# The opening of a decoder layer: identity transposes while x loads, a shorter bias table with its block part copied on VectorE, earlier row factors, and a DRAM spread cut in 16 pieces

## Chip, cores and metric

The kernel runs on one core of one Trainium2 chip. The metric is device time in microseconds (us) of one execution; lower is better. Runs of one kernel differ a little, so times are compared as medians of several.

## The reference

One layer of a decoder with S = 512 tokens and D = 2048 columns, batch 1, all in float32. A normalized input goes through an attention mixer with 16 heads in 4 groups, is added back, and a SwiGLU block (2048 to 2 x 5632 and back) follows, with a last norm:

```python
hn = rmsnorm(h, mix_norm_g[i])
h = h + nsa_mixer(hn, rel_bias, nsa_w_in[li], nsa_w_out[li], ...)
h = h + swiglu(rmsnorm(h, ffn_norm_g[i]), ffn_w_in[i], ffn_w_out[i])
return rmsnorm(h, final_norm_g)
```

The mixer projects hn to queries, to keys and values of three branches (compressed blocks, selected blocks, window) and to gates. Keys and values of the compressed branch go through a small MLP over blocks of 32 tokens with stride 16. Each score gets a bias that depends on the head and on a bucket of the distance between query and key: `rel_bias[rel_bucket(dist)]`, with 32 buckets. With 512 tokens every block is selected and the window covers all, so selected and window branches both see all keys up to the query.

## The kernel before, in words

All matrix products are split in two parts each: a value x becomes a high part (a rounded copy, ACT) and a low part (x minus the high part, VectorE, called DVE in the profile), and `three` (L264) issues three matmuls for a product: high x high, low x high, high x low (L265 to L267).

**Weights.** The class `Weights` (L63) holds a list of weight pieces, most of 512 KB, in the order of use. `load` (L72) issues a DMA on SP into one of three `raw` buffers; `split` (L82) makes `whi` on ACT (L95) and `wlo` on VectorE (L96) in one of four buffers; `take` gives out the next piece and `ahead(n)` splits until n pieces are ready, then issues loads until three more are on their way. A load can go out only when the split of the piece three places before has freed its `raw` buffer. Every engine works through its own instructions in the order in which the program lists them.

**Opening (L360 to L480).** The input x is loaded as four tiles of 128 tokens, in four column quarters, on SP and ACT's queue. PE transposes x into chunks of 128 columns (16 chunks in all). Each chunk is scaled by the norm's gain: ACT makes `hn_h` (L400), VectorE `hn_l` (L401). The row factor of the norm (one over the root mean square of a token) isn't applied here; it is multiplied into the outputs of the projections. The first four chunks are made before the first projection (L439, then `scaled_in`). The first projection (`ws`, 24 matmuls for a weight piece) then runs in four quarters `q`; in quarters 0 to 2 the next four chunks are made between its matmuls (`chunk`, L392), so each chunk is used one quarter later. The table `side` names further work of a quarter:

- `square(i)` (L406): ACT squares half a token tile and sums it, for the row factors; eight of them.
- `pos_turn`: two small transposes.
- `table(c0, c1)` (L414): the bias table `tab`, made by a matmul of the 33 x 16 biases with a one-hot matrix `oh` and copied by VectorE. Columns 0 to 639 hold the bias for the distances 511 down to -128; 16 x 62 further columns hold, for each of 16 offsets b, the distances 465 + b - 16 n. They are made in four parts of 512, 128, 496 and 496 columns.
- `factors` (L419): a chain of small VectorE instructions with one Sqrt on ACT; it ends with `diag` (L429), a diagonal matrix of the row factors.

After quarter 3, PE multiplies ones by `diag` (L468), and ACT copies the result to `ybc` (L469), the row factors of all tokens in every partition. Then POOL writes `tab` to DRAM (`d_t`, L472, and `d_c`, L473), reads the compressed branch's bias back in eight DMAs (L475), and issues the spread: `d_u` (L479) gets 128 copies of the 10240 values of `d_t`, in four DMAs of 2560 columns. Much later each head's bias tile `tb` is read from `d_u` by one DMA on SP (L726).

**Then** (L533 to L550): the second and third projection of 256 columns each (4 weight pieces each), and a loop of four turns, each with one projection piece (`ws`) and two pieces of the first MLP (`mlp1`), all of which pass through `Weights`. The text calls this loop the first MLP stretch. Behind it come the other projections, the attention, the output product and the SwiGLU block, which the change doesn't touch.

PSUM tiles of the opening come from `bank`, which takes turns between the names "tr" and "mlp", two buffers each.

Of the kernel before, what the change touches and what calls it, by code (L numbers as in the profile page):

```python
# [10 lines left out]
F32 = mybir.dt.float32  # L11
F32R = mybir.dt.float32r
I32 = mybir.dt.int32
AF = mybir.ActivationFunctionType
# [24 lines left out]
TP_GAP, HN_GAP = 40, 48  # L39
RESYNC = 14  # L40
SPREAD = 2560


def _bucket_onehot():
# [127 lines left out]
def nsa_block(ctx: ExitStack, tc: tile.TileContext, x, rel_bias, mix_g, ffn_g, fin_g, w_in, w_out,  # L172
# [111 lines left out]
    def run(gen):  # L284
        for _ in gen:
            pass
# [61 lines left out]
    with ExitStack() as st1:  # L348
# [4 lines left out]
        def proj_tiles(n=2):  # L353
            return [(ps1 if next(turns) % 4 > 1 else psx).tile([128, 512], F32, name="proj") for _ in range(n)]
# [5 lines left out]
        with ExitStack() as st0:  # L360
# [3 lines left out]
            g16 = xp.tile([KC, 128], F32, name="g16")  # L364
            gcol = xp.tile([128, KC], F32, name="gcol")
            relt = xp.tile([NB + 1, H], F32, name="relt")
            oh = xp.tile([NB + 1, UL + 16 * CL], F32, name="oh")
            ones = xp.tile([128, 128], F32, name="ones")
            diag = xp.tile([128, NT, 128], F32, name="diag")
            nc.scalar.dma_start(g16, mix_g.rearrange("o (k p) -> (o k) p", p=128))  # L370
            for q in range(4):
                if q < RAW:
                    W.load()
                for t in range(NT):
                    eng = nc.scalar if q < 2 and t % 2 else nc.sync
                    eng.dma_start(xt[t][:, 512 * q:512 * (q + 1)], x[tok(t), 512 * q:512 * (q + 1)])
                if q == 0:
                    act(warm, epsc, AF.Sqrt)
                if q == 1:
                    nc.sync.dma_start(oh, onehot)  # L380
            pool.dma_start(pos[:, 0], pos_k)
            pool.dma_start(pos[:, 1], pos_v)
            pool.dma_start(relt[:NB, :], rel_bias)
# [5 lines left out]
            def bank(shape):  # L389
                return ps1.tile(shape, F32, name=next(names))  # L390
# [13 lines left out]
            def square(i):  # L404
                t, c = i % NT, i // NT
                act(junk, xt[t][:, 1024 * c:1024 * (c + 1)], AF.Square, accum_out=ssq[:, t, c:c + 1])  # L406
# [7 lines left out]
            def table(c0, c1):  # L414
                p = bank([H, 512])
                mm(p[:, :c1 - c0], relt, oh[:, c0:c1], start=True, stop=True)
                dve.tensor_copy(tab[:, c0:c1], p[:, :c1 - c0])

            def factors():  # L419
# [9 lines left out]
                dve.tensor_tensor(diag, ident.unsqueeze(1).to_broadcast([128, NT, 128]),  # L429
                                  ymul.unsqueeze(2).to_broadcast([128, NT, 128]), op=OP.mult)  # L430

            p = bank([128, KC])
            nc.tensor.transpose(p, g16, ident[:KC, :KC])
            dve.tensor_copy(gcol, p)
# [5 lines left out]
            for k in range(4):  # L440
                scaled_in(k, ps[k])
            ps = proj_tiles()
            cuts = ((0, 512), (512, UL), (UL, UL + 496), (UL + 496, UL + 992))
            side = [[lambda: square(0)], [pos_turn, lambda: square(1), lambda: square(2), lambda: table(*cuts[0])],
                    [lambda: square(3), lambda: square(4), lambda: table(*cuts[1]), lambda: square(5),
                     lambda: table(*cuts[2]), lambda: table(*cuts[3])],
                    [lambda: square(6), lambda: square(7), factors]]
            for q in range(4):
                it = ws(ps, q, W.take(0))
                next(it)  # L450
                if q < 3:
                    W.split()
                else:
                    W.ahead(1)
                for f in side[q]:
                    f()
                for _ in range(4):
                    next(it)
                if q == 3:
                    W.ahead(2)  # L460
                for k in range(4 * q + 4, 4 * q + 8):
                    if q < 3:
                        chunk(k)
                    if k % 4 < 3:
                        next(it)
                run(it)
            p = bank([128, S])
            mm(p, ones, diag.rearrange("p t c -> p (t c)"), start=True, stop=True)  # L468
            act(ybc, p, AF.Copy)  # L469
            ps_kc0 = ps  # L470
            W.ahead(3)
            pool.dma_start(d_t, tab[:, :UL])  # L472
# [1 line left out]
            for a in range(8):  # L474
                pool.dma_start(biasc[16 * a:16 * a + 16],  # L475
                               bass.AP(tensor=d_c.tensor, offset=d_c.offset + 7 - a,
                                       ap=[[CL, 16], [16 * CL, H], [1, 55]]))
            for c0 in range(0, H * UL, SPREAD):
                pool.dma_start(d_u[:, c0:c0 + SPREAD], bass.AP(tensor=d_t.tensor, offset=d_t.offset + c0,  # L479
                                                               ap=[[0, 128], [1, SPREAD]]))  # L480

        cp = st1.enter_context(tc.tile_pool(name="cp", bufs=1))
        blk_h = cp.tile([128, 32, G, 32], F32R, name="blk_h")
# [10 lines left out]
        def kv_out(ps, g0):  # L494
            return lambda u: dve.tensor_tensor(kvT[:, g0 + u], ps[u], ybc, op=OP.mult)
# [11 lines left out]
        def mlp1(ps, gi, g):  # L507
            for k in range(4):
                i = 4 * gi + k
                three(ps, blk_h[:, i].rearrange("p g c -> p (g c)"), blk_l[:, i].rearrange("p g c -> p (g c)"),  # L510
                      g[0][:, k], g[1][:, k], i == 0, i == 31)
# [21 lines left out]
        ps = proj_tiles()  # L533
        for i in range(4):
            run(ws(ps, i, W.take(), end=kv_out(ps, 2)))
        ps = proj_tiles()
        for i in range(4):
            run(ws(ps, i, W.take()))
            build_blk(0, i)
        W.ahead(3)  # L540
        for u in range(2):
            kv_out(ps, 0)(u)
        ps, hk = proj_tiles(), ps1.tile([128, 256], F32, name="mlp")
        for i in range(4):
            run(ws(ps, i, W.take(), end=kv_out(ps, 2)))
            mlp1(hk, 2 * i, W.take())
            mlp1(hk, 2 * i + 1, W.take())
        W.ahead(3)
        hid = gelu(hk)
        ps = proj_tiles()  # L550
# [883 lines left out]
```

## Time and profile before

| what | value |
|---|---|
| time, median of 3 runs | 2171.51 us (2167.26 to 2173.09) |
| profiled execution, its own time | 2174.41 us |
| its span | 2172.7 us |
| granted TensorE clock, mean | 0.996 |
| busy: PE, weight loads, VectorE, ACT, POOL | 2141.7, 1984.1, 1580.9, 928.3, 54.5 us |
| DMA traffic | 344.14 MB, mean 158 GB/s |

The profile is of one execution. A row of the timeline gives start and duration in us, engine, line, instruction, what it writes and reads, how many were merged, and in square brackets how long the engine had been idle and what ended that. Matmul durations overlap, since matmuls are pipelined: their distance is read from their starts. PEld is the weight load of a matmul. SPq, ACTq and POOLq are DMA issues. A row of a view by stretches gives the stretch, its length, then the busy us of PE, PEld, DVE, ACT and POOL with the number of instructions, the granted clock, the mean busy share of the 16 DMA engines and GB/s. A row of the waits names who waited on what for whom: total us, times, longest. A row of the DMA queues gives packets, MB and share of the 16 engines.

### The profile page before, as it was taken

The numbers are of one execution on the slowest core, as the hardware profiler recorded it, in microseconds if no ns is written. First come the engines' busy times: TensorE is split into PE (matmuls) and PEld (weight loads), VectorE is DVE, ScalarE is ACT, GpSimd is POOL, SyncE is SP. The second block draws the span as 40 slices with busy tenths as digits, with TensorE's granted clock in tenths as the row PEclk, the third lists the DMA queues.
The fourth block names the chain that finished last, engine by engine and source line by source line (L and its number), as shares of the span: only waits on it lengthen the run. The fifth ranks groups of instructions, "written<-read, shape, count | busy, mean of one in ns | idle before, by whom it ended". The sixth has DMA issues, their size and how long they took to land.

```text
span 2172.7 us, 37012 instructions
## 1 busy us (share of the span) xinstructions
PE 2141.7 (99%) x15061; PEld 1984.1 (91%) x15061; DVE 1580.9 (73%) x2602; ACT 928.3 (43%) x1433; POOL 54.5 (3%) x110
## 2 busy tenths in 40 slices
PE   8999999999999999999999999999999999999998
PEld 6789798988989988899999999999999888989996
DVE  4565666666665446798888888888888677877785
ACT  5343454454444324343434434343443444544353
POOL 2000000000000000000000000000000000001000
PEclk9999999999999999999999999999999999999999
DMA  7546223223253543344344334334433776878894
GB/s 234 159 126 168 84 83 98 88 83 97 88 199 117 201 139 117 105 138 125 119 127 137 125 119 127 120 124 126 137 120 124 248 265 207 292 276 306 308 327 152
DMA packets 240998, 344.14 MB, mean 158 GB/s; under 512 B 13067, under 2 KB 179003, under 8 KB 239676
## 3 DMA queue, kind: packets, MB, share of 16 engines
q1 hardware_dynamic: 226108, 267.51, 39.1%
q0 software_dynamic: 12816, 70.06, 8.5%
q10 hardware_dynamic: 1904, 4.20, 0.5%
q8 instruction: 118, 1.93, 0.4%
q14 instruction: 52, 0.43, 0.1%
HBM read 298.64 MB, written 48.34 MB: 160 GB/s over the span
## 4 chain that ended last, share of the span: by engine, by line
PE 93%; DMA 3%; DVE 2%; ACT 1%; issue 0%; POOL 0%; SPq 0%; ACTq 0%; DVEq 0%; POOLq 0%
PE f L267 18%; PE f L265 18%; PE f L266 18%; PE proj L265 8%; PE proj L267 8%; PE proj L266 8%; PE pt L776 2%; DMA raw<-in_nsa_w_in 1%; PE pp L267 1%; PE pp L266 1%; PE pp L265 1%; PE o L266 1%; PE o L267 1%; PE s L265 1%; PE o L265 1%; PE po L265 1%
## 5 line engine op out<-in xcount | busy, mean ns | idle before, releaser
L96 DVE TENSOR_TENSOR wlo<-raw,whi 128x1024 fp32r<-128x1024 f32 (+1 forms) x226 | 272.7, 1209 | 142.7 <-ACT whi L95 141.1
L95 ACT ACTIVATE whi<-raw 128x1024 fp32r<-128x1024 f32 (+1 forms) x226 | 234.9, 1041 | 240.5 <-DVE raw L933 124.7
L933 DVE TENSOR_TENSOR tlo<-tt,thi 128x1536 fp32r<-128x1536 f32 (+2 forms) x135 | 197.2, 1461 | 112.2 <-ACT thi L1035 88.6
L265 PE MATMUL f<-hn_h,whi 128*128 128x256 f32 x984 | 272.1, 277 | 0.8 <-ACT E L993 0.8
L266 PE MATMUL f<-hn_l,whi 128*128 128x256 f32 x984 | 272.1, 277 | 0.0
L267 PE MATMUL f<-hn_h,wlo 128*128 128x256 f32 x984 | 272.0, 276 | 0.0
L1030 ACT ACTIVATE whi<-raw 128x1024 fp32r<-128x1024 f32 x123 | 126.0, 1057 | 292.3 <-DVE raw L933 282.1
L265 PE MATMUL proj<-hn_h,whi 128*128 128x512 f32 x512 | 206.0, 402 | 4.8 <-ACT whi L95 4.3
L267 PE MATMUL proj<-hn_h,wlo 128*128 128x512 f32 x512 | 202.1, 395 | 0.0
L266 PE MATMUL proj<-hn_l,whi 128*128 128x512 f32 x512 | 201.1, 393 | 0.3 <-DVE hn_l L401 0.3
L265 PEld LDWEIGHTS f<-hn_h,whi 128*128 128x128 f32 x984 | 184.7, 188 | 1.2 <-ACT E L993 1.2
L267 PEld LDWEIGHTS f<-hn_h,wlo 128*128 128x128 f32 x984 | 184.8, 188 | 0.0
L266 PEld LDWEIGHTS f<-hn_l,whi 128*128 128x128 f32 x984 | 184.7, 188 | 0.0
L1035 ACT ACTIVATE thi<-tt 128x1536 fp32r<-128x1536 f32 x82 | 121.9, 1486 | 84.1 <-PE f L266 84.1
L933 DVE TENSOR_TENSOR wlo<-raw,whi 128x1024 fp32r<-128x1024 f32 x123 | 147.1, 1223 | 0.0
L265 PE MATMUL proj<-whi,hn_h 128*128 128x256 f32 (+2 forms) x496 | 146.6, 296 | 0.0
L267 PE MATMUL proj<-whi,hn_l 128*128 128x256 f32 (+2 forms) x496 | 145.6, 293 | 0.0
L266 PE MATMUL proj<-wlo,hn_h 128*128 128x256 f32 (+2 forms) x496 | 145.3, 293 | 0.0
L267 PE MATMUL f<-whi,tlo 128*128 128x512 f32 x320 | 125.9, 394 | 1.4 <-DVE tlo L933 1.4
L265 PE MATMUL f<-whi,thi 128*128 128x512 f32 x320 | 125.4, 392 | 1.9 <-ACT thi L1152 1.9
L291 DVE TENSOR_TENSOR ptl<-pt,pth 128x128 fp32r<-128x128 f32 (+3 forms) x128 | 62.5, 488 | 88.8 <-ACT pth L290 88.7
L266 PE MATMUL f<-wlo,thi 128*128 128x512 f32 x320 | 125.6, 393 | 0.0
(318 smaller groups left out, 6118.0 us busy)
## 6 DMA issues: line engine op xcount, KB each, us to landing
raw<-in_ffn_w_in SPq DMA_DIRECT2D x135, 512.0 KB, 3.7
raw<-in_ffn_w_out SPq DMA_DIRECT2D x88, 512.0 KB, 5.5
raw<-in_nsa_w_in SPq DMA_DIRECT2D x48, 512.0 KB, 3.8
rawx<-in_ffn_w_in SPq DMA_DIRECT2D x41, 512.0 KB, 4.8
raw<-in_nsa_w_out SPq DMA_DIRECT2D x32, 512.0 KB, 4.2
rawx<-d_a SPq DMA_DIRECT2D x31, 512.0 KB, 4.7
raw<-in_nsa_w_in SPq DMA_DIRECT2D x56, 256.0 KB, 3.1
ah<-d_s POOLq DMA_DIRECT2D x16, 896.0 KB, 7.4
```

The lines of the kernel that those rows point to most:

```text
L95: self.nc.scalar.activation(hi[:, :n], src, AF.Copy)
L96: self.nc.vector.tensor_tensor(lo[:, :n], src, hi[:, :n].bitcast(F32), op=OP.subtract)
L265: mm(o, ah, bh, start=start, stop=False, skip_group_check=True)
L266: mm(o, ah, bl, start=False, stop=False, skip_group_check=True)
L267: mm(o, al, bh, start=False, stop=stop, skip_group_check=True)
L291: dve.tensor_tensor(lo, psum_ap, hi.bitcast(F32), op=OP.subtract)
L776: nc.tensor.transpose(pt[rows, 128 * (t - kt):128 * (t - kt + 1)], src, ident)
L933: dve.tensor_tensor(o, a, b, op=OP.subtract)
L1030: act(h, r, AF.Copy)
L1035: act(h, ttf, AF.Copy)
```

## The change

Four edits, all in the opening and the two stages behind it:

- 24 transposes of the identity into a PSUM tile of their own stand first on PE. They need only `ident`.
- The one-hot matrix and its load shrink to the first 640 columns. The two table parts of 496 columns go; both remaining parts are made in quarter 1. In quarter 2 `by_blocks` fills the block part: POOL sets the columns of negative distance, VectorE copies 16 rows of 38 values, each with a step of 16 columns, out of the first part.
- The squares stand in quarters 0 to 2 (two, three, three), `factors` at the start of quarter 3 ahead of the split of the next weight piece. The ones x `diag` matmul stands within quarter 3's code. It still follows the 24 matmuls of the quarter, and precedes the same later work.
- The spread is cut in 16 DMAs of 640 columns (320 KB each), issued on SP in place of POOL: one behind each weight piece of the second and third projections, two in each turn of the first MLP stretch.

`ahead(1)` takes the place of `split()` in the first three quarters; the loads that it issues follow on SP in the same order as before.

```diff
-SPREAD = 2560
+SPREAD, N_WARM = UL, 24
...
-            oh = xp.tile([NB + 1, UL + 16 * CL], F32, name="oh")
+            oh = xp.tile([NB + 1, UL], F32, name="oh")
...
-                    nc.sync.dma_start(oh, onehot)
+                    nc.sync.dma_start(oh, onehot[:, :UL])
...
+            def by_blocks():
+
+                t = tab[:, UL:].rearrange("p (b n) -> p b n", n=CL)
+                pool.memset(t[:, :, 38:], NEG)
+                for b in range(16):
+                    u = 511 - (465 + b)
+                    dve.tensor_copy(t[:, b, :38], tab[:, u:u + 16 * 37 + 1:16])
+
+            p = bank([128, 512])
+            for i in range(N_WARM):
+                nc.tensor.transpose(p[:, 128 * (i % 4):128 * (i % 4 + 1)], ident, ident)
...
-            cuts = ((0, 512), (512, UL), (UL, UL + 496), (UL + 496, UL + 992))
-            side = [[lambda: square(0)], [pos_turn, lambda: square(1), lambda: square(2), lambda: table(*cuts[0])],
-                    [lambda: square(3), lambda: square(4), lambda: table(*cuts[1]), lambda: square(5),
-                     lambda: table(*cuts[2]), lambda: table(*cuts[3])],
-                    [lambda: square(6), lambda: square(7), factors]]
             for q in range(4):
                 it = ws(ps, q, W.take(0))
                 next(it)
-                if q < 3:
-                    W.split()
-                else:
-                    W.ahead(1)
-                for f in side[q]:
-                    f()
+                if q == 3:
+                    factors()
+                W.ahead(1)
+                if q == 1:
+                    pos_turn()
+                    table(0, 512)
+                    table(512, UL)
+                if q == 2:
+                    by_blocks()
+                for i in ((0, 1), (2, 3, 4), (5, 6, 7), ())[q]:
+                    square(i)
                 for _ in range(4):
                     next(it)
...
+                if q == 3:
+                    p = bank([128, S])
+                    mm(p, ones, diag.rearrange("p t c -> p (t c)"), start=True, stop=True)
+                    act(ybc, p, AF.Copy)
                 run(it)
-            p = bank([128, S])
-            mm(p, ones, diag.rearrange("p t c -> p (t c)"), start=True, stop=True)
-            act(ybc, p, AF.Copy)
...
-            for c0 in range(0, H * UL, SPREAD):
-                pool.dma_start(d_u[:, c0:c0 + SPREAD], bass.AP(tensor=d_t.tensor, offset=d_t.offset + c0,
-                                                               ap=[[0, 128], [1, SPREAD]]))
+
+            def spread_steps():
+                for c0 in range(0, H * UL, SPREAD):
+                    nc.sync.dma_start(d_u[:, c0:c0 + SPREAD], bass.AP(tensor=d_t.tensor, offset=d_t.offset + c0,
+                                                                      ap=[[0, 128], [1, SPREAD]]))
+                    yield
+
+            spread = spread_steps()
...
         for i in range(4):
             run(ws(ps, i, W.take(), end=kv_out(ps, 2)))
+            next(spread)
...
         for i in range(4):
             run(ws(ps, i, W.take()))
             build_blk(0, i)
+            next(spread)
...
         for i in range(4):
             run(ws(ps, i, W.take(), end=kv_out(ps, 2)))
+            next(spread)
             mlp1(hk, 2 * i, W.take())
             mlp1(hk, 2 * i + 1, W.take())
+            next(spread)
```

## The prediction

> **What bounds the kernel now.** I read the page first, then the waits of PE, then the chain of waits and the timeline around the longest of them.
>
> ```profile
> PE 2141.7 (99%) x15061; PEld 1984.1 (91%) x15061; DVE 1580.9 (73%) x2602; ACT 928.3 (43%) x1433; POOL 54.5 (3%) x110
> ...
> PE proj L265 <- ACT whi L95: 4.3, 1, 4.3
> ...
> raw<-in_nsa_w_in SPq DMA_DIRECT2D x48, 512.0 KB, 3.8
> ...
> d_u<-d_t POOLq DMA_DIRECT2D x4, 1280.0 KB, 16.0
> ```
>
> PE is the bound: of a span of 2172.7 us it is idle for 31. So only PE time counts: an idle stretch, PE work that goes, or PE work at a low clock. The change touches the first 75 us and the spread that runs there. The largest wait of PE is the second row, 4.3 us on a weight piece. The last two rows are DMA issues with their KB and median us to landing. The chain of waits says what stood behind the 4.3 us:
>
> ```profile
> 40.43 24.17 DMA raw<-in_nsa_w_in
> ```
>
> This weight load takes 24.17 us from issue to landing, where the median is 3.8. The DMA view of 52 to 60 us shows with whom it shared the engines:
>
> ```profile
> q0 software_dynamic: 253, 2.12, 78.7%
> q1 hardware_dynamic: 264, 0.27, 16.0%
> ```
>
> The columns are packets, MB and share of 16 engines. q0 is POOL's queue and carries the four spread DMAs (L479); q1 is SP's and carries the loads. In 8 us each queue moved about 260 packets, but a spread packet is 8.4 KB on the mean and a load packet 1.0 KB. The engines take packets in turn, so the load gets 0.27 MB in 8 us and stands until the spread (four times 1280 KB, 5.24 MB) is through. The clock then makes it dearer:
>
> ```profile
> 61.04 0.39 PE L267 MATMUL proj<-hn_h,wlo 128*128 128x512 f32 x1
> 65.73 0.80 PE L265 MATMUL proj<-hn_h,whi 128*128 128x512 f32 x1 [4.30 <-ACT whi L95]
> ...
> 71.42 0.49 PE L265 MATMUL proj<-hn_h,whi 128*128 128x512 f32 x1
> ...
> 45.13 0.40 PE L266 MATMUL proj<-hn_l,whi 128*128 128x512 f32 x1
> ...
> 66.00:68.00 2.00, 1.96 (x4) 1.07 (x5) 1.55 (x2) 1.34 (x2) 0.00 (x0) 0.50 0.07 23
> 72.00:74.00 2.00, 2.00 (x10) 1.65 (x9) 1.49 (x2) 0.00 (x0) 0.00 (x0) 1.00 0.83 254
> ```
>
> The last two rows are from the view by stretches: the granted clock is 0.50 behind the stall and 1.00 again at 72. From 45.13 to 61.04 lie 70 matmuls, 0.227 us each. From 61.04 to 71.42 lie 13, which should take 2.95 us and take 10.38. **The stall costs 7.4 us**, 4.3 of it idle and the rest slow clock and restart.
>
> **The change part by part.**
>
> *Spread in 16 pieces on SP.* It takes away the 10 KB packets that shared with the loads: each piece is 128 rows of 2.56 KB in SP's own queue, issued once or twice in a weight step, behind loads that are already on their way. A piece has no row in the trace, so I bound it. By the q0 row a MB costs 0.787 x 16 x 8 / 2.12 = 47.5 engine-us, by the q1 row 75.9. The piece of 0.328 MB over 16 engines is then 0.97 to 1.55 us. A line through the two (0.398 us for 8.4 KB, 0.078 us for 1.0 KB) gives 0.144 us for 2.56 KB, so 8 rows for each engine take 1.15 us; I take 1.2. The first eight pieces fall to one in 24 matmuls (5.5 us), beside one load of 512 KB: no crowd. The last eight fall in the first MLP stretch, two in each turn of one projection piece and two MLP pieces:
>
> ```profile
> 101.52 1.06 ACT L95 ACTIVATE whi<-raw 128x1024 fp32r<-128x1024 f32 x1 [4.38 <-PE proj L266]
> ...
> 126.27 1.06 ACT L95 ACTIVATE whi<-raw 128x1024 fp32r<-128x1024 f32 x1 [4.15 <-PE proj L266]
> 100.00:120.00 20.00, 20.00 (x121) 17.86 (x120) 8.26 (x7) 7.79 (x8) 0.00 (x0) 1.00 0.60 183
> ```
>
> Three turns in 24.75 us are 8.25 us each; a DMA share of 0.60 is 4.95 us of a turn, and two pieces make it 7.35. That fits, up to 1.65 us a piece. The added wait: the first piece waits on SP for d_t to land, with all later weight loads behind it. POOL issues d_t once the 128 wide table part is copied; that part moves from the third quarter to the second, so d_t lands some 10 us earlier than now, and SP comes to the first piece only behind loads of the second projection, later than the one of 40.43. I count nothing. What is late next, once the stall is gone? ACT and VectorE split three weight pieces ahead, and for 74 to 200 us the list of PE's waits is empty. So the 7.4 us are taken whole. If the cover were gone, the price would be the stall again.
>
> *Bias table of 640 distances.* Two table matmuls go, and the 128 wide one moves a quarter earlier:
>
> ```profile
> 28.27 0.40 PE L267 MATMUL proj<-hn_h,wlo 128*128 128x512 f32 x1
> 28.60 0.39 PE L416 MATMUL mlp<-oh,relt 33*16 33x128 f32 x2
> 28.83 0.99 PE L416 MATMUL tr<-oh,relt 33*16 33x496 f32 x2
> ...
> 30.58 0.50 PE L265 MATMUL proj<-hn_h,whi 128*128 128x512 f32 x1
> ```
>
> From 28.27 to 30.58 are 2.31 us for one matmul and the tables; without them 0.23; 0.23 come back for the part that moves: **1.85 us**. VectorE gets 16 copies of 16x38 in place of two of 16x496. They stand ahead of hn_l of the last four chunks, which PE needs in the last quarter:
>
> ```profile
> 29.67 1.23 DVE L96 TENSOR_TENSOR wlo<-raw,whi 128x1024 fp32r<-128x1024 f32 x1 [0.19 <-ACT whi L95]
> 31.01 0.65 DVE L417 COPY tab<-tr 16x496 f32<-16x496 f32 x1
> 31.59 0.65 DVE L417 COPY tab<-mlp 16x496 f32<-16x496 f32 x1
> ...
> 0.87 0.06 DVE L208 MEMSET epsc<- 128x1 f32 x1 [0.87 <-PEq L1418]
> ...
> 32.85 0.18 ACT L406 ACTIVATION_READ_ACCUMULATOR junk<-x 128x1 f32 x1
> ```
>
> A copy of 16x38 is not in the trace. Bounds: 0.06 us (the memset) and 0.20 (the distance of the small instructions at 41.40 and 41.59, below). I take 0.20, so 3.2 us against the 1.3 that go. VectorE is free from 30.8, when wlo is done. ACT ends its three squares at 33.05 and only then makes hn_h (0.69 us), so hn_l can't begin before 33.75; the copies end at 34.0. At four times 0.69 (ACT) or 0.75 (VectorE) the last hn_l ends near 36.9; PE, 2.1 us earlier than now, asks for it near 37.3. The cover is 0.4 us: tight, but it holds at the dear bound. POOL's memset is done long before. The load of the one-hot matrix shrinks by 0.13 MB, behind the first x; nothing waits for it now.
>
> *Row factors within the last quarter.* PE ends the quarter, waits for diag and goes on:
>
> ```profile
> 42.58 0.39 PE L267 MATMUL proj<-hn_h,wlo 128*128 128x512 f32 x1
> 43.96 1.10 PE L468 MATMUL tr<-diag,ones 128*128 128x512 f32 x2 [0.99 <-DVE diag L429]
> ...
> 38.23 0.75 DVE L401 SCALAR_TENSOR_TENSOR hn_l<-mlp,gcol,hn_h 128x512 fp32r<-128x512 f32 x1 [0.38 <-ACT hn_h L400]
> 41.40 0.16 DVE L420 TENSOR_REDUCE ytmp<-ssq 128x4 f32<-128x8 f32 x1 [0.99 <-ACT junk L406]
> 41.59 0.17 DVE L421 TENSOR_SCALAR ytmp<-ytmp 128x4 f32<-128x4 f32 x1
> 43.12 0.69 DVE L429 TENSOR_TENSOR diag<-ident,ymul 128x512 f32<-128x512 f32 x1
> ```
>
> 42.81 would be in time; 43.96 is 1.15 late. The factors take 2.4 us (41.40 to 43.81). Begun at 36.9 behind the last hn_l they end at 39.3, and PE, early by 2.1, asks at 40.7: **the 1.15 us go**. The added wait is ACT's: its Sqrt waits for ytmp, with the split of the next weight piece behind it. That whi ends near 38.8, its wlo (1.23) behind diag near 40.5; PE needs it past the ybc matmul, near 41.8. Two squares move from ACT's last quarter to its first two, 1.2 us in each, where it now idles about as long ahead of the next chunk, so they cost nothing:
>
> ```profile
> 15.87 0.69 ACT L400 ACTIVATE hn_h<-mlp,gcol 128x512 fp32r<-128x512 f32 x1 [1.11 <-PE mlp L396]
> ...
> 24.59 0.69 ACT L400 ACTIVATE hn_h<-mlp,gcol 128x512 fp32r<-128x512 f32 x1 [1.45 <-PE mlp L396]
> ```
>
> *Identity transposes.* Now the transposes of x run cold:
>
> ```profile
> 1.08 0.29 POOL masks.py:199 TENSOR_SCALAR_AFFINE_SELECT ident<-ident 128x128 f32<-128x128 f32 x1
> 7.05 0.48 PE L439 MATMUL mlp<-ident,x 128*128 128x128 f32 x1 [2.88 <-DMA x<-in_x]
> 9.00 0.18 PEld L439 LDWEIGHTS mlp<-ident,x 128*128 128x128 f32 x1 [0.39 <-DMA x<-in_x]
> 9.91 0.41 PE L439 MATMUL mlp<-ident,x 128*128 128x128 f32 x1
> ...
> 10.27 0.27 PE L439 MATMUL mlp<-ident,x 128*128 128x128 f32 x1
> 10.38 0.27 PE L439 MATMUL tr<-ident,x 128*128 128x128 f32 x1
> ```
>
> The four transposes of the third x tile take 0.91 us (9.00 to 9.91, 0.23 each); two at the end are 0.11 apart. The 24 new ones start near 1.5 us, when ident is made, and end by 7.0 even if all are slow, as the first x arrives (7.05). The third tile lands at 9.00 whatever PE does. Behind it four transposes take 0.46 in place of 0.91, and the first of the last tile 0.27 in place of 0.41: **0.6 us**, between 0 (the clock falls back while PE waits for x) and 0.6. ACT and the first matmuls follow it.
>
> The sum: 7.4 + 1.85 + 1.15 + 0.6 = **11.0 us**. The profiled execution took 2174.41 us (span 2172.7), so it would take 2163.4. It lies 2.9 us above the median of the runs, 2171.51, from which the forecast is **2160.5**. Behind the last piece, near 125 us, nothing else changes, and PE sets the pace there, so the gain reaches the end.
>
> **The rivals.**
>
> *The stall stays.* The spread still moves 5.24 MB in the same stage; if pieces and loads crowd each other as now, 7.4 of the 11.0 us are lost: 2167.9. For it: the engines are the same 16. Against it: the load's 24 us come from sharing turn by turn with 8 KB packets, and a piece ahead in its own queue costs it some 1.2 us. The Trainium skill, "DMA: Bandwidth & Descriptors", section "Issuing engines are not separate DMA queues", speaks for it: transfers of all issuing engines end on the same 16 engines and interleave, so moving one saves only issue time. By that sentence alone the time would be that of this rival; its section "Queues, rings and completion order" (a turn is one packet of one queue) fits the two queue rows instead.
>
> *VectorE becomes the wait of the last quarter.* If the strided copies take 0.4 us each, hn_l of the last chunk is 3.2 us later, less 0.4 of cover: 2.8 us come back, 2163.3. For it: the cover is thin. Against it: 38 elements is little, and no small VectorE row above is over 0.17.
>
> *The pieces fill the DMA engines in the MLP stretch: slower.* As the dear end I take the landing of d_u's transfers, 16 of 20 of them the reads of 256 KB into tb (L726):
>
> ```profile
> DMA to landing us min/median/max: 2.6/3.7/22.6
> ```
>
> At 4.6 us a piece (3.7 us for 256 KB, made larger to 320 KB), a turn is 4.95 + 9.2 = 14.2 us against 8.25. Four turns lose 23.6 us. Of the three weight pieces split ahead I count the projection piece, 5.5 us, as cover: 18.1 are left against 11.0 gained, 2178.6. It decides against the change from 4 x (2c - 3.3) - 5.5 = 11, c = 3.7 us a piece. For it: all 128 rows of a piece read the same 2.56 KB. Against it: now all rows read the same 10 KB and move 265 GB/s (2.12 MB in 8 us), and 3.7 us is mostly latency. The skill's same page, section "Bandwidth", advises transfers of 1 MiB and up; its table (0.95 us for 64 KB, 6.15 for 1 MB) gives, as an estimate, 2.3 us a piece. By that a turn would be 9.6 us, and four would lose 5.4, about the cover; no row of this trace shows it.
>
> **How the numbers follow.** Forecast 0.74, stall stays 0.09, VectorE 0.12, DMA-bound stretch 0.05. A difference under 0.3% (6.5 us) can't be told from no change here. Faster by more, below 2165.0: the forecast and VectorE, less the 0.01 that scatter takes, 0.85; within: the stall stays and that 0.01, 0.10; slower 0.05. The range: down from 2160.5 by the scatter of the runs (4.3 below their median) and 1 for the terms, 2155; up to the VectorE case with 1.6 of scatter and 1 for the terms, 2166. That leaves out the other two rivals, 0.14, and a little at the ends.
>
> **What would show it.** Right: no PE wait over 1 us between 35 and 80 us, no clock under 1.00 at 66, loads that land in under 8 us, PE at its second projection near 41 instead of 44.5. Wrong: a load of over 15 us again (first rival), PE waits on hn_l near 37 us (second), ACT waits on raw of several us and PE waits on whi between 95 and 130 us (third). Transposes still 0.2 us apart behind 7 us would strike the last term.

## The result and the profile after

| | before | after |
|---|---|---|
| time, median (range, runs) | 2170.32 us (2167.26 to 2173.09, 4) | 2158.77 us (2158.44 to 2159.27, 4) |
| ratio, 95% interval | | 0.9952 (0.9941 to 0.9964) |
| span of the profiled execution | 2172.7 us | 2156.7 us |

The change is faster by 0.48%, 10.4 us by the ratio. Further runs of the kernel before, beside the experiments, had medians of 2168.62, 2169.13 and 2168.74 us (20, 9 and 19 runs), and the changed kernel run once more had 2158.66 us, ratio 0.9957 (0.9944 to 0.9969). The gain is about 10 us. The spans differ by 16.0; that is not the gain, and the last point of the section on the prediction says why.

The page after has PE busy as before, with 5.4 us less, and one row that the prediction did not look at, the queue `q8`:

```profile
span 2156.7 us, 37078 instructions
PE 2136.3 (99%) x15081; PEld 1983.8 (92%) x15081; DVE 1580.3 (73%) x2616; ACT 927.9 (43%) x1433; POOL 52.8 (2%) x107
...
q8 instruction: 118, 1.93, 0.4%
```

The waits of PE after (us in total, times, longest). The row of 4.3 us on a weight piece is gone, and so is the wait for `diag`. What is new at the top is a wait of the attention for `mx`, the VectorE operation that adds the bias (L773, L752 before). Its row of before comes first, then the rows after:

```profile
PE s L265 <- DVE mx L752: 2.7, 4, 1.4
```

```profile
PE s L265 <- DVE mx L773: 3.9, 4, 1.9
PE tr L450 <- DMA x<-in_x: 1.8, 2, 1.1
PE tr L442 <- POOL ident masks.py:199: 1.4, 1, 1.4
```

The timeline of PE after, in the opening (L442 are the identity transposes, L450 those of x, L479 is ones x `diag`):

```profile
1.42 4.67 PE L442 MATMUL tr<-ident 128*128 128x128 f32 x24 [1.42 <-POOL ident masks.py:199]
...
7.34 0.33 PE L450 MATMUL tr<-ident,x 128*128 128x128 f32 x1 [1.08 <-DMA x<-in_x]
...
10.00 0.27 PE L450 MATMUL mlp<-ident,x 128*128 128x128 f32 x1
10.72 0.50 PE L265 MATMUL proj<-hn_h,whi 128*128 128x512 f32 x1 [0.45 <-ACT hn_h L400]
...
28.08 0.40 PE L267 MATMUL proj<-hn_h,wlo 128*128 128x512 f32 x1
28.31 0.40 PE L265 MATMUL proj<-hn_h,whi 128*128 128x512 f32 x1
...
40.19 0.39 PE L267 MATMUL proj<-hn_h,wlo 128*128 128x512 f32 x1
40.41 1.02 PE L479 MATMUL mlp<-diag,ones 128*128 128x512 f32 x2
40.87 0.79 PE L265 MATMUL proj<-hn_h,whi 128*128 128x512 f32 x1
```

x's transposes lie 0.11 us apart from the second on; the tables' hole behind 28.08 is closed; L479 follows the last matmul of the quarter without a wait; the second projection begins at 40.87 in place of 44.49, which is this row of before:

```profile
44.49 0.80 PE L265 MATMUL proj<-hn_h,whi 128*128 128x512 f32 x1
```

VectorE after, at the same place (its row of 16 merged copies, the last hn_l, the first row of the factors, `diag`):

```profile
30.62 1.70 DVE L438 COPY tab<-tab 16x38 f32<-16x38 f32 x16
...
35.84 0.75 DVE L401 SCALAR_TENSOR_TENSOR hn_l<-tr,gcol,hn_h 128x512 fp32r<-128x512 f32 x1 [0.32 <-ACT hn_h L400]
36.51 0.15 DVE L420 TENSOR_REDUCE ytmp<-ssq 128x4 f32<-128x8 f32 x1
...
38.22 0.68 DVE L429 TENSOR_TENSOR diag<-ident,ymul 128x512 f32<-128x512 f32 x1
```

And the view by stretches after, in the place of the stall and in the first MLP stretch (last three columns: granted clock, DMA share, GB/s):

```profile
66.00:68.00 2.00, 2.00 (x10) 1.67 (x9) 1.09 (x1) 1.83 (x2) 0.00 (x0) 1.00 0.75 227
...
100.00:120.00 20.00, 20.00 (x119) 17.78 (x119) 11.58 (x13) 9.10 (x9) 0.00 (x0) 1.00 0.93 255
```

The clock at 66 us is 1.00, it was 0.50; the DMA share of the MLP stretch has gone from 0.60 to 0.93.

**Two distances serve as rulers below.** The *opening* runs from the first projection matmul to the first instruction on `kcc_h` (the compressed keys, made behind the first MLP stretch). The *attention start* runs from there to the first write to `d_o`, the mixer's output. Both are starts in one trace, so what x's landing scatters (the first matmul came at 10.2 to 11.2 us in these traces) is not in them. Each is read from the one profiled execution of its kernel. The rows of `kcc_h` and `d_o`, of before and then of after (first and last start in us):

```profile
L290 ACT ACTIVATE kcc_h<-tr x1: 279/279/279, 158.5 to 158.5; 128x128 fp32r<-128x128 f32 x1
L803 SPq DMA_DIRECT2D d_o<-of x24: 338/338/339, 257.4 to 615.9; - x24
```

```profile
L290 ACT ACTIVATE kcc_h<-tr x1: 278/278/278, 147.2 to 147.2; 128x128 fp32r<-128x128 f32 x1
L824 SPq DMA_DIRECT2D d_o<-of x24: 338/338/342, 247.5 to 605.8; - x24
```

| kernel | opening | attention start | median (range, runs) | ratio (95%) |
|---|---|---|---|---|
| before | 147.4 | 98.9 | 2170.32 | |
| after | 136.5 | 100.3 | 2158.77 | 0.9952 (0.9941 to 0.9964) |
| e1, only the spread in pieces | 139.7 | 99.1 | 2163.40 (2161.06 to 2165.85, 9) | 0.9976 (0.9966 to 0.9986) |
| e2, spread as before | 146.4 | 101.4 | 2168.97 (2167.65 to 2170.72, 10) | 1.0003 (0.9993 to 1.0012) |
| e3, 16 pieces on POOL | 137.3 | 100.8 | 2159.54 (2158.51 to 2164.19, 4) | 0.9962 (0.9947 to 0.9977) |
| e4, 4 lumps on SP | 138.8 | 100.3 | 2162.41 (2160.47 to 2163.95, 6) | 0.9973 (0.9961 to 0.9984) |
| e5, changed kernel again | 136.5 | 100.9 | 2158.66 (2158.19 to 2161.25, 5) | 0.9957 (0.9944 to 0.9969) |
| e6, no identity transposes | 136.5 | 99.1 | 2158.62 (2158.29 to 2160.46, 5) | 0.9955 (0.9943 to 0.9968) |
| e7, 32 of them | 136.6 | 100.2 | 2159.40 (2158.19 to 2161.41, 5) | 0.9959 (0.9945 to 0.9973) |
| e8, 16 of them | 136.6 | 99.0 | 2157.83 (2157.52 to 2160.50, 5) | 0.9953 (0.9940 to 0.9965) |
| e9, factors as before | 137.7 | 100.8 | 2161.16 (2160.76 to 2164.84, 5) | 0.9971 (0.9959 to 0.9983) |
| e10, long table | 138.5 | 100.2 | 2162.06 (2161.40 to 2162.84, 7) | 0.9970 (0.9959 to 0.9981) |
| e11, every piece twice | 142.4 | 100.2 | 2165.04 (2164.01 to 2167.91, 10) | 0.9986 (0.9977 to 0.9995) |
| e12, first bias tile read early | 136.5 | 98.4 | 2158.47 (2156.80 to 2159.04, 5) | 0.9954 (0.9941 to 0.9966) |

e1 to e4, e5 to e8 and e9 to e12 each ran together, against 2168.62, 2169.13 and 2168.74 us.

### The profile page after: what moved, and what is told of

Read it like the earlier page. It is cut to its first block, busy times and chain, and to the rows that moved or that the text cites. A ratio compares the mean times of both kernels' runs of the same rounds, so it can differ in the third digit from the quotient of the medians.

```text
span 2156.7 us, 37078 instructions
## 1 busy us (share of the span) xinstructions
PE 2136.3 (99%) x15081; PEld 1983.8 (92%) x15081; DVE 1580.3 (73%) x2616; ACT 927.9 (43%) x1433; POOL 52.8 (2%) x107
## 3 DMA queue, kind: packets, MB, share of 16 engines
q8 instruction: 118, 1.93, 0.4%
## 4 chain that ended last, share of the span: by engine, by line
PE 97%; DVE 1%; ACT 1%; DMA 1%; issue 0%; SPq 0%; ACTq 0%; DVEq 0%
PE f L266 19%; PE f L267 19%; PE f L265 19%; PE proj L265 8%; PE proj L267 8%; PE proj L266 8%; PE pt L797 2%; PE pp L265 1%; PE pp L266 1%; PE pp L267 1%; PE o L266 1%; PE o L267 1%; PE s L265 1%; PE o L265 1%; PE po L267 1%; PE po L265 1%
```

## The experiments

### The spread: which part of the edit does it (e1 to e4)

**e1** is the kernel before with only the spread changed to 16 pieces on SP, at the places that the change has.

```diff
-SPREAD = 2560
+SPREAD = UL
...
-            for c0 in range(0, H * UL, SPREAD):
-                pool.dma_start(d_u[:, c0:c0 + SPREAD], bass.AP(tensor=d_t.tensor, offset=d_t.offset + c0,
-                                                               ap=[[0, 128], [1, SPREAD]]))
...
+            spread = spread_steps()
...
+            next(spread)
```

> The kernel before with one edit, the spread cut in 16 pieces on SP. My theory: the 10 KB packets of the spread shared the engines with the loads, so this edit alone takes the whole stall, 7.4 to 7.7 us: about 2162.7 us, no PE wait on a weight piece, the 1.0 us wait for diag stays. Rival (the spread crowds the loads wherever it is issued): a PE wait of several us on a weight piece stays or moves, about 2166 to 2170 us.

Measured: 2163.40 us, 5.2 us less than before (3.0 to 7.4 by the interval). In its trace the clock at 66 us is 1.00 and from 11 to 160 us PE waits for weights nowhere; its one wait of 1 us there is the old one for `diag`. The opening is 7.7 us shorter, just past the end of that interval; it compares one execution of each kernel. So the stall goes with this edit alone.

**e2** is the changed kernel with the old spread, four transfers of 1280 KB on POOL; **e3** has all 16 pieces on POOL, one behind the other where the four stood; **e4** has the four big transfers on SP at that place.

```diff
...
-            spread = spread_steps()
+            for c0 in range(0, H * UL, 2560):
+                pool.dma_start(d_u[:, c0:c0 + 2560], bass.AP(tensor=d_t.tensor, offset=d_t.offset + c0,
+                                                             ap=[[0, 128], [1, 2560]]))
...
-            next(spread)
```

This is e2; in e3 640 (UL) stands for 2560, in e4 nc.sync for pool.

> The changed kernel with the spread as before: four transfers of 2560 columns on POOL. Theory: the stall ends when the spread's data are through, and the spread starts at a time set by POOL's own chain (near 39.8 us in both kernels). So PE, 3.6 us earlier by the other edits, only waits longer: idle near 8 us, restart near 65.7 us as before, and the time is that of the kernel before, about 2170 us. Rival (the edits add up): 7.6 us over the changed kernel, about 2166.4 us, idle 4.3 us.

> The changed kernel with 16 pieces of 640 columns, but on POOL and all at once where the four stood. Theory (queues take turns by packets, so a load's share goes by packet size): a load of 32 rows for each engine takes turns with packets of 2.56 KB, 32 x (0.144 + 0.078) = 7.1 us, so it lands near 48 us in place of 64 and PE does not wait: 2159 to 2160 us. Rival (what counts is the bytes in flight, 5.24 MB at once): loads of about 20 us and the stall of the run with four transfers, 2166 to 2170 us.

> The changed kernel with four transfers of 2560 columns at once, as before, but on SP. Theory (a queue works in order): the loads issued ahead land in 4 us; the next load, issued near 47 us, lands only behind the whole spread, near 62 us, but PE needs it near 73 us: no PE wait, 2159 to 2160 us. Rival (a lump of 5.24 MB stalls PE in whatever queue, and the cutting in pieces is what helps): a PE wait of several us on a weight piece between 57 and 75 us, 2164 to 2170 us.

Measured, from the chains of waits and the timeline of each (issue to landing of a weight load; then PE). e2:

```profile
40.32 22.98 DMA raw<-in_nsa_w_in
...
64.43 0.79 PE L265 MATMUL proj<-hn_h,whi 128*128 128x512 f32 x1 [6.57 <-ACT whi L95]
```

e3:

```profile
39.91 7.84 DMA raw<-in_nsa_w_in
50.12 17.18 DMA raw<-in_nsa_w_in
```

e4:

```profile
48.07 20.82 DMA raw<-in_nsa_w_in
```

e2 takes the time of before (2168.97), though table and factors still do their part: PE comes to the missing weight 3.6 us earlier (64.43 - 6.57 = 57.86, in before 65.73 - 4.30 = 61.43), but then stands 6.57 us (near 8 were expected). The stall ends with the spread, and swallows most of what was gained ahead of it: PE goes on 1.3 us earlier than in before. **The edits do not add**: the spread is worth 7.7 us of opening to the kernel before (e1) and 9.9 to the changed one (e2 against after), and table and factors are worth 3.2 behind the spread's edit (e1 against after) but 1.0 without it (before against e2).

e3 has the same bytes on the same queue of POOL, and PE never stands for more than 0.3 us. The load that took 22.98 takes 7.84. So POOL's queue need not stall PE, if what is issued at once is small. Two things differ from e2 there, and e3 doesn't part them: a packet of POOL's queue is smaller (between 40 and 70 us 5.56 MB in 1411 packets, against 5.61 MB in 734), and POOL issues eight pieces at once and waits for the landing of earlier ones before it issues the rest (its issues go on from 39.4 to 55.6 us), so fewer bytes stand in the queue at once. A load that is issued in the middle still takes 17.18, hidden by the pieces split ahead.

e4 is the other half: nothing shares with the load turn by turn, but the lumps stand ahead of it in the same queue, and it takes 20.82. PE does not stand for weights, since this hits a later load with more work split ahead; it waits 1.3 us for `blk_h` and `blk_l`, and the opening is 2.3 us longer than after. Neither the forecast of e4 (2159 to 2160 us) nor its rival (2164 to 2170) has its time, 2162.41. So either half of the edit alone takes most of the 9.9 us: pieces alone (e3) leave 0.8 us of opening and SP's queue alone (e4) 2.3; the change does both, and spaces the pieces.

### The identity transposes and what they shift (e5 to e8, e12)

e5 is the changed kernel unchanged, for scatter; e6, e7 and e8 change the number of transposes.

```diff
-SPREAD, N_WARM = UL, 24
+SPREAD, N_WARM = UL, 0
```

This is e6; e7 has 32, e8 16.

> The changed kernel once more, as the measure for the next three. Theory on the 1.3 us that it lost at the start of the attention: a 16 KB packet of PE's instruction fetch (queue q8) falls on one DMA engine while the first bias tile tb is read, so tb lands in 4.6 us in place of 3.2 and PE waits 1.9 us in place of 0.7. It must come again at the same place in every execution: tb lands in 4.5 to 4.8 us, q8 packet 1.5 to 2.0 us behind its issue. Rival (scatter of one execution): tb lands in about 3.3 us here. Time about 9.9 us under the kernel before, 2158 to 2159 us.

> The changed kernel without the 24 identity transposes. Two theories give two terms: without them the transposes of x run slow again (first matmul of the projection 0.4 us later, near 11.1 us in place of 10.7); and PE has 48 instructions less, so its fetch comes near 9.6 us later against the code and leaves the first tb read alone (tb lands in 3.2 us, PE waits 0.7 us in place of 1.9): 0.4 - 1.3, so 0.9 us under the changed kernel. Rival (the fetch has nothing to do with it): tb lands in 4.6 us and the time is 0.4 us over the changed kernel.

> The changed kernel with 32 in place of 24 identity transposes. Theory: they end near 7.0 us, still ahead of x, so the first matmul stays at 10.7 us; PE's fetch comes 3.2 us earlier against the code, ahead of the tb read, which lands in 3.2 us: 1.3 us under the changed kernel, the best of the four. Rival (the fetch has nothing to do with it): no difference, tb 4.6 us.

> The changed kernel with 16 in place of 24 identity transposes. Theory: PE's fetch comes 3.2 us later against the code, behind the tb read, which lands in 3.2 us. The 16 end near 4.5 us; if 3.1 us of work are enough to raise the clock and 2.8 us of idling do not lower it, the first matmul stays at 10.7 us (1.3 us under the changed kernel), else it comes at 11.1 us (0.9 us under). Rival (the fetch has nothing to do with it): tb lands in 4.6 us.

The timelines of PE. e6 (none), whose first x tile lands as in after (7.36, there 7.34):

```profile
7.36 0.48 PE L450 MATMUL tr<-ident,x 128*128 128x128 f32 x1 [3.63 <-DMA x<-in_x]
7.63 0.42 PE L450 MATMUL mlp<-ident,x 128*128 128x128 f32 x1
...
11.22 0.50 PE L265 MATMUL proj<-hn_h,whi 128*128 128x512 f32 x1
```

e8 (16):

```profile
1.43 3.67 PE L442 MATMUL tr<-ident 128*128 128x128 f32 x16 [1.43 <-POOL ident masks.py:199]
...
6.85 0.47 PE L450 MATMUL tr<-ident,x 128*128 128x128 f32 x1 [1.53 <-DMA x<-in_x]
7.12 0.42 PE L450 MATMUL mlp<-ident,x 128*128 128x128 f32 x1
```

With x at the same time, 24 transposes bring the first projection matmul from 11.22 to 10.72: 0.5 us. In e8 sixteen do nothing for the clock: x's transposes stay about 0.21 apart. With 32 they are 0.11 apart, as with 24. But 24 is not safely enough. With 24 or 32, the distance of PE's transposes falls from 0.21 to 0.11 us at 5.0 (e5) to 7.2 us (e9, e11), though all start at 1.42 to 1.43. In after it is at 5.2, behind the 18th, and only the last six lie 0.11 apart. In e4, e9 and e11 all 24 are slow, and x's transposes became fast just in time. This is the row of e9, 5.38 us where after has 4.67:

```profile
1.43 5.38 PE L442 MATMUL tr<-ident 128*128 128x128 f32 x24 [1.43 <-POOL ident masks.py:199]
```

The times of e5 to e8 lie within 1.6 us and cannot be told apart; the gains of 0.9 to 1.3 us that were expected of e6 to e8 don't show in them. The ruler says why the gain of the transposes does not show either: the attention start is 99.1 with none and 99.0 with 16, but 100.2 to 100.9 with 24 and 32. Something there takes back 1.1 to 1.9 us.

What it is shows in VectorE's first rows with the bias tile `tb`, first in after and then in e8:

```profile
208.94 0.69 DVE L773 CUSTOM_DVE_ANT_0 p<-s,tb 128x512 f32<-128x512 f32 x1 [1.72 <-DMA tb<-d_u]
```

```profile
207.79 0.69 DVE L773 CUSTOM_DVE_ANT_0 p<-s,tb 128x512 f32<-128x512 f32 x1 [0.49 <-DMA tb<-d_u]
```

VectorE waits 1.2 us longer for `tb`, and PE behind it 1.94 in place of 0.71 (0.68 before). The DMA views from the issue of `tb` on (packets, MB, share of 16 engines; last column us to landing), of after (204.2 to 209 us) and of e8 (204.3 to 207.9 us):

```profile
q1 hardware_dynamic: 1199, 0.79, 59.8%
q8 instruction: 1, 0.02, 1.5%
...
tb<-d_u SPq DMA_DIRECT2D x1, 256.0 KB, 4.6
```

```profile
q1 hardware_dynamic: 1196, 0.78, 76.2%
...
tb<-d_u SPq DMA_DIRECT2D x1, 256.0 KB, 3.4
```

In after one packet of q8 falls beside the read of `tb`: 1.5% of 16 engines for 4.8 us is 1.15 us on one engine, and `tb` lands 1.2 us later. (A packet of q14 comes 3.8 to 4.3 us behind the issue, in before too.) By the page q8 has 118 packets and 1.93 MB in all, 16.4 KB each, and PE's 15081 matmuls and 15081 weight loads are 256 for each packet. I read it as the fetch of PE's instructions; that it is PE's is argued from this count, not shown. That the packet is what delays `tb` rests on its place: in the traces of before, e1, e6 and e8 it comes 5.9 to 9.8 us behind the issue of `tb`, which lands after 3.2 to 3.4 us; in after, e2 to e5, e7 and e9 to e11 it comes 1.1 to 1.9 us behind, and `tb` lands after 4.5 to 4.8. No run takes the packet alone away. e7 was meant to move it out ahead of `tb` and didn't: 1.1 us behind the issue in place of 1.6.

The longer wait can cost clock too: in e2, e3, e7, e9 and e10 the granted clock falls to 0.50 for 3.4 us close behind it (at 211 us in e7), in after, e4, e5 and e11 it doesn't. The attention start doesn't tell the two groups apart (100.2 to 101.4 and 100.2 to 100.9).

**e12** takes the wait away: the first head's `tb` is read at 181 us instead of 204, into a buffer of its own, so that no late landing can matter.

```diff
+        TB0 = keep.tile([128, S], F32, name="tb0")
+        nc.sync.dma_start(TB0, bass.AP(tensor=d_u.tensor, offset=d_u.offset + 127, ap=[[H * UL - 1, 128], [1, S]]))
         hid = gelu(hv)
...
-        load_bias(0)
+        TB[0] = TB0
         pump(-1, 9.7)
```

> The changed kernel with the first bias tile tb read into a buffer of its own, ahead of the first query projection, some 20 us earlier. Theory (the 1.3 us lost at the start of the attention are the late landing of this one read): VectorE's wait for tb goes whole, PE's first wait there falls from 1.9 us to about 0.2, and the time is 1.7 us under the changed kernel, near 2157.0 us, wherever the instruction fetch falls. Rival (VectorE's own chain sets that start): PE's wait stays above 1 us and the time is that of the changed kernel.

In its timeline VectorE's row has no wait any more:

```profile
206.89 0.69 DVE L775 CUSTOM_DVE_ANT_0 p<-s,tb 128x512 f32<-128x512 f32 x1
```

The attention start is 98.4, 1.9 less than in after and 0.5 less than in before: the loss was the wait for `tb`, whole. The time, 2158.47 us, can't be told from 2158.66, though 1.7 us less were expected: such a step is below the scatter of five runs, and no version here is shown to beat the changed kernel.

### The other terms, one at a time (e9 to e11)

**e9** puts squares and factors back to the last quarter as before; **e10** makes the block part by table matmuls again (both of 496 columns, in quarter 2) and no copies; **e11** issues each piece twice, the second into a buffer `d_v` that nothing reads.

```diff
-                if q == 3:
-                    factors()
                 W.ahead(1)
...
-                for i in ((0, 1), (2, 3, 4), (5, 6, 7), ())[q]:
+                for i in ((0,), (1, 2), (3, 4, 5), (6, 7))[q]:
                     square(i)
+                if q == 3:
+                    factors()
```

```diff
-            oh = xp.tile([NB + 1, UL], F32, name="oh")
+            oh = xp.tile([NB + 1, UL + 16 * CL], F32, name="oh")
...
-                    nc.sync.dma_start(oh, onehot[:, :UL])
+                    nc.sync.dma_start(oh, onehot)
...
-                    by_blocks()
+                    table(UL, UL + 496)
+                    table(UL + 496, UL + 992)
```

```diff
+    d_v = dram.tile([128, H * UL], F32, name="d_v")
...
                     nc.sync.dma_start(d_u[:, c0:c0 + SPREAD], bass.AP(tensor=d_t.tensor, offset=d_t.offset + c0,
                                                                       ap=[[0, 128], [1, SPREAD]]))
+                    nc.sync.dma_start(d_v[:, c0:c0 + SPREAD], bass.AP(tensor=d_t.tensor, offset=d_t.offset + c0,
+                                                                      ap=[[0, 128], [1, SPREAD]]))
```

> The changed kernel with squares and factors where they stood before (one, two, three, two squares; factors behind the split in the last quarter). Theory: diag is ready 5.6 us behind the last hn_h, as before, near 41.4 us, and PE asks for it at 40.4: a wait of about 1.0 us, 1.1 us over the changed kernel, 2159.8 us. Rival (with a shorter third quarter ACT is already late, and the order of the squares no longer matters): no wait for diag, 2158.7 us.

> The changed kernel with the block part of the bias table made as before, by two matmuls and two copies of 496 columns in the third quarter, from the full one-hot matrix. Theory: PE does 1.85 us more there (two table matmuls of 0.83 us and the turn between kinds), 2160.6 us. Rival (the copies on VectorE delay the last chunks, so the edit is worth less than its matmuls): under 1 us over the changed kernel.

> The changed kernel with each of the 16 pieces issued twice (the second to a DRAM tensor that nothing reads), 10.5 MB in all. It measures how near the first MLP stretch is to its DMA bound. From the changed kernel's DMA share of 0.93 a turn of 8.25 us holds 4.95 us of loads and two pieces of 1.36 us; with four pieces it is 10.4 us, 2.15 over in each of four turns, 8.6 less 5.5 us of pieces split ahead: about 3 us over the changed kernel, with PE waits on weight pieces near 110 us (0.5 us if a piece costs 1.2, 6 us if 1.55). Rival (the share counts engines that wait, and there is room for twice as much): no PE wait, within 0.5 us.

PE's timelines of e9, then of e10:

```profile
41.26 1.10 PE L479 MATMUL mlp<-diag,ones 128*128 128x512 f32 x2 [0.99 <-DVE diag L429]
```

```profile
27.77 0.40 PE L267 MATMUL proj<-hn_h,wlo 128*128 128x512 f32 x1
28.09 1.00 PE L416 MATMUL mlp<-oh,relt 33*16 33x496 f32 x2
28.93 0.99 PE L416 MATMUL tr<-oh,relt 33*16 33x496 f32 x2
29.86 0.50 PE L265 MATMUL proj<-hn_h,whi 128*128 128x512 f32 x1
```

The wait for `diag` is back in e9 and the opening is 1.2 us longer. In e10 the tables take 2.09 us (27.77 to 29.86) where one matmul takes 0.23, and the opening is 2.0 longer. The times rise by more, 2.5 and 3.4 us over e5, but with intervals of about 2.6 us either way; the rulers are the better measure.

e11 takes 2165.04 us, 6.4 more than e5, the opening 5.9 more. The view by stretches and the timeline of PE:

```profile
100.00:110.00 10.00, 10.00 (x62) 8.95 (x61) 4.07 (x4) 3.19 (x3) 0.00 (x0) 1.00 1.01 345
...
120.00:130.00 10.00, 10.00 (x46) 8.24 (x45) 4.88 (x9) 4.13 (x6) 0.00 (x0) 1.00 1.03 254
```

```profile
118.27 0.50 PE L268 MATMUL proj<-hn_h,wlo 128*128 128x512 f32 x1 [0.20 <-DVE wlo L96]
142.65 0.41 PE L266 MATMUL proj<-whi,hn_h 128*128 128x304 f32 x1 [0.80 <-DVE yt L318]
146.12 0.41 PE L266 MATMUL proj<-whi,hn_h 128*128 128x304 f32 x1 [2.37 <-DVE yt L318]
```

The 16 engines are full (1.01, 1.03), yet in the MLP stretch PE waits only 0.2 us: what was split ahead covers it. The bill comes 20 us later. ACT and VectorE split late (a `wlo` that begins at 117.91 in after begins at 123.76, 3.81 of it waiting for `whi`), VectorE's further work behind it is late, and PE waits 3.2 us for `yt` at 142 to 146; from 140 to 150 us the granted clock is 0.86.

What a piece takes can be read from its packets. In after its 16 pieces are 2048 packets of 2.56 KB, 0.123 us each on the mean: 0.98 us of the 16 engines a piece. Between 100 and 120 us are 512 of them, 0.153 us each: 1.2 a piece. In the traces with single pieces it is 0.92 to 1.23, over all pieces or in this stretch, and in e11 1.2. The 1.36 us of e11's expectation puts the whole rise of the DMA share, from 0.60 to 0.93, to the pieces; their packets make 0.25 of it, and the rest is other traffic in that stretch. With 1.2 us a piece and 4.95 us of loads, four pieces make 9.75 us in a turn of 8.25, so the engines overfill all the same.

## Why the prediction was right, point by point

- **The stall, 7.4 us.** The stall gave 7.7 (openings of before and e1), the clock stayed at 1.00, loads of the second projection landed within 5.6 us of their issue. The reading of the chain (a load held by the spread, idle and low clock together) was right. The term belongs to this kernel's whole, not to the edit: e2 shows that it hides gains ahead of it.
- **First rival, the stall stays.** It fell with e1 and e3. The Trainium skill, "DMA: Bandwidth & Descriptors", section "Issuing engines are not separate DMA queues", says that issuing from several engines saves only issue time. With 16 pieces the trace agrees nearly: SP in place of POOL is worth 0.8 us of opening (e3 against after, which also spaces them). With the four lumps it doesn't: SP in place of POOL makes the opening 7.6 us shorter (146.4 in e2, 138.8 in e4): there the lumps stand behind three loads and meet a later one. The turn of one packet per queue, in the Trainium skill's "Queues, rings and completion order" on the same page, agrees with the 253 and 264 packets of before. In e3 it stays open: the 7.1 us expected took packets of 2.56 KB, but the trace has 1024 of 5.12 KB, 0.25 us each, for which the same sum gives 9.7 us, and between 42 and 48 us q1 moved 688 packets against 320 of q0. That 7.84 came near 7.1 is luck.
- **The table, 1.85 us.** The matmul behind the tables comes at 28.31 in place of 30.58, 2.27 earlier; 0.38 of this PE had from the start (10.72 for 11.10), which leaves 1.89. e10 gives 2.0.
- **VectorE as the wait of the last quarter.** It fell: 16 copies take 1.70 us, 0.106 each, between the bounds of 0.06 and 0.20, at the cheap one's side. The last hn_l begins at 35.84 and the factors at 36.51, 0.4 earlier than reckoned.
- **The factors, 1.15 us.** 42.58 to 43.96 has become 40.19 to 40.41: 1.16 us. e9 gives 1.2. With 7.7, 1.89 and 1.16 the opening's 10.9 are accounted for but 0.1; `ahead(1)` in place of `split()` has no run of its own.
- **The identity transposes, 0.6 us.** 0.5 by e6 and after with x landing alike; 0.38 between before and after, whose first x came 0.3 us later. The size hangs on x's landing. That the clock does not fall back in the 1.08 us in which PE waits for x was the open end of the range, and held. That 24 transposes reach the higher clock before x comes was taken for granted; in e4, e9 and e11 they didn't, though x's own transposes were fast.
- **"The gain reaches the end."** This is the step that failed, by 1.4 us. To `kcc_h` the gain is 11.3 us (10.9 in the opening, 0.4 ahead of it); at the first write to `d_o` it is 9.9. No late engine stood behind the last piece in the trace of before, and the prediction left it at that; but the first read of `tb` came to wait, 1.2 us longer, where a packet of `q8` now falls beside it.
- **DMA-bound MLP stretch.** It fell as a loss: no PE wait there. The 1.2 us a piece of the prediction held (0.98 on the mean, 1.2 in this stretch); the share of 0.93 leaves little, but only 0.25 of its rise by 0.33 is the pieces. The table in the section "Bandwidth" of the Trainium skill's "DMA: Bandwidth & Descriptors" gave 2.3 us as an estimate. The trace doesn't agree: no trace has more than 1.23. e11 shows the mechanism, at 6.4 us in place of 3 and with the wait in another place than foretold.
- **The number.** 2160.5 stood on a median of 2171.51; more runs put the kernel before near 2169, and the gain is 9.9 by the ruler (10.4 by the times, whose interval of 7.8 to 12.8 holds 11 too). Both errors are small and of opposite sign, so that 2160.5 came within 1.7 us of 2158.77 is partly luck. The spans differ by 16.0 because the profiled execution of before had lost 5.7 us elsewhere: the stretch from 1709 us on, in the SwiGLU block, which the change doesn't touch, took 289.9 us to its last read of the residual, and 284.2 both in after and in e1. Its view by stretches:

```profile
1740.00:1760.00 20.00, 18.48 (x114) 16.17 (x112) 10.69 (x17) 7.23 (x9) 1.61 (x3) 1.00 0.94 325
1760.00:1780.00 20.00, 19.06 (x102) 16.30 (x103) 18.16 (x29) 10.71 (x15) 0.54 (x1) 0.91 0.73 248
```

PE stands for 2.5 us in 40 there and the clock falls to 0.91, beside DMA engines 0.94 full; after has PE busy throughout. Why that execution stood there was not tried.

## What to carry to other kernels

When a load takes many times its median, look at what stands on the DMA engines beside it: a background transfer of some MB that isn't urgent belongs in small pieces between the urgent loads. A stall whose end is set by a transfer swallows most of a gain made ahead of it, so remove it first, and don't add up edits measured beside it. When a step of a microsecond or two is to be judged, measure it by distances within a trace, between points that the edit does and doesn't touch; the total time here scatters by as much.

## What was not expected of the hardware

- A single packet of 16.4 KB in the queue of kind `instruction` took about 1.1 us on one DMA engine, and in the nine traces where it falls beside a transfer of 256 KB this lands after 4.5 to 4.8 us in place of 3.2 to 3.4. Where it falls moves with the program: without the 24 transposes (e6) it comes 9.6 us behind the issue of `tb`, with them (after, e5) 1.4 to 1.6.
- Sixteen transposes, 3.67 us of PE work that ended 1.5 us before x came, left the clock low. With 24 the last six already ran at 0.11 us in after (4.67 in all) and the clock held through an idle 1.08 us; in e4, e9 and e11 all 24 were slow (5.38).
- Whether `tb` could be read straight from `d_t`, with no spread at all, was not tried: it needs a negative step between partitions.
